# A hybrid decoder layer on one core: a PSUM tile for each accumulating bank, and the last norm's squares summed by TensorE

## The chip, the cores and the metric

One core of a Trainium2 chip runs the whole layer as one program. The metric is device time in microseconds (us) of one execution; a median of several runs is given. The profile is of one further execution. TensorE appears twice in it: PE is the products, PEld the loads of the stationary operand, which overlap them. DVE is VectorE, ACT is ScalarE, POOL is GpSimd, SP issues the DMAs.

## The reference, cut to what matters

512 prompt tokens and 8 single sample tokens pass one layer of width 1024:

```
h = x + Mixer(RMSNorm(x));  h = h + SwiGLU(RMSNorm(h));  y = RMSNorm_final(h)
swiglu(xn) = (silu(xn @ w_a) * (xn @ w_b)) @ w_ffn_out        hidden width 2816
rmsnorm(x, g) = x * rsqrt(mean(x*x over the 1024 features) + eps) * g
```

The change touches the second product of the SwiGLU (with `w_ffn_out`) and the final norm. The mixer (retention, dilated attention, gates) stays as it is.

## The kernel before

Everything is feature-major: a tile holds 128 features on its partitions and 520 columns, which are two halves of 260 (256 prompt tokens and 4 sample tokens each). A float32 product is made of three products of shortened operands: weight and activation are each split into a high and a low part (`wh`, `wl`; `xh`, `xl`), and high·high, high·low and low·high are added in PSUM. ACT makes each `wh` (L195), DVE makes `wl = raw - wh` (L198). `advance(t)` issues these splits up to six blocks ahead of TensorE, in program order; six buffers each for `wh` and `wl` are reused.

PSUM has eight banks. The pool `pmain` has two buffers, tag `pm`, each of shape [128, 2, 512], so two banks a buffer; the pool `pside` has three one-bank buffers for transposes and small sums (`sbank`, tiles named `sp`) and one more bank (`abank`, tag `acc`). The order of the instructions on each engine is the order of the program text; the framework adds the semaphore waits from what tiles the instructions read and write.

**The FFN's second product, first two chunks.** The hidden width is cut into chunks of 8, 8 and 6 tiles. For the first two chunks a pair of 2 x 2 blocks is multiplied with seven products instead of eight (a Strassen-like scheme). `ffn_out(c)` for c = 0, 2, 4, 6 calls `quad` (L268), which runs seven groups of 12 products: 8 calls in all, four behind each chunk. The list `SEVEN` says which PSUM bank each group adds to: 0, 1, 0, 2, 0, 1, 0. Banks 0 and 1 are the two halves of one `pm` tile; bank 2 is the `acc` bank, named `pc`. After groups 1, 2, 3 and 5 ACT copies the bank as it then stands into SBUF (L288, the snapshots `s12`, `s35`); after groups 4, 5, 6 and 7 `evac` has DVE add banks and snapshots into `hT` (L1239 to L1247), the residual stream in SBUF. So a bank is read while its sum is still open, and written again by a later group.

**The last chunk and the final norm.** The last six hidden tiles go through plain products: output tiles c = 0 and 1 interleaved (`LAST`), then 2 and 3 (`unit`, L245), then c = 4 to 7 for the first half of the columns (f = 0) and again for the second (f = 1), at L1354. There a `pm` tile is taken for two values of c, one bank each. `ev_f` (L1323, DVE) adds each result to `hT`.

For the final norm each tile is turned token-major. `fin_T` makes three PE transposes (L307) into two `sp` buffers: 2 x 128 prompt tokens and 4 sample tokens. `fin_sq` squares and sums them on ACT with an accumulator (L1279, L1281: three activations, each with a read of the accumulator). `fin_g` (DVE, L1285, L1287) multiplies by the norm's weight into `yt` and `ys`. A generator `gen_final` does this for one c; `pump`, called after each product step, advances the generators by one step, `drain` runs them to their end. `fin_out(f)` adds the eight partial sums (L1302, L1304), makes 1/rms (`rstd_rows`: DVE L314, a power on POOL, L316), scales `yt` (L1312 on DVE, L1310 on ACT) and issues the output DMAs. The first half's `fin_out(0)` stands with a drain inside the f = 1 pass, the second's at the end.

Of the kernel before, what the change touches and what calls it, by code (L numbers as in the profile page):

```python
# [8 lines left out]
F32 = mybir.dt.float32  # L9
F32R = mybir.dt.float32r  # L10
AF = mybir.ActivationFunctionType
ALU = mybir.AluOpType
AX = mybir.AxisListType
# [4 lines left out]
T, NS, C, D = 512, 8, 520, 1024  # L18
HF, HT = 260, 256
# [13 lines left out]
def tile_hybrid_layer(  # L33
# [9 lines left out]
    V, A, G_, PE, SP = nc.vector, nc.scalar, nc.gpsimd, nc.tensor, nc.sync  # L43
# [5 lines left out]
    pmain = ctx.enter_context(tc.tile_pool(name="pmain", bufs=2, space=PSUM))  # L49
# [39 lines left out]
    ones1 = cst[:, 272:273]  # L89
# [173 lines left out]

    SEVEN = ((0, 0), (1, 3), (0, 4), (2, 1), (0, 5), (1, 2), (0, 6))

    def quad(xh, xl, snap, evac):

        s = pos[0] // 8  # L268
        pos[0] += 16
        nkp = QUADS[s]  # L270
        pm = pmain.tile([128, 2, 512], F32, tag="pm", name="pm")
        out = [pm[:, 0, :HF], pm[:, 1, :HF], None]
        begun = set()
        for j, (bank, x) in enumerate(SEVEN):
            advance(bid[s, 0] + j)
            if bank == 2:
                out[2] = abank("pc")[:, :HF]
            h, l = split[bid[s, 0] + j]
            for k in range(nkp):
                ks = slice(k * 128, k * 128 + 128)  # L280
                for w, r in ((h, xh), (h, xl), (l, xh)):
                    PE.matmul(out[bank], w[:, ks], r[:, k, x, :], start=bank not in begun, stop=k == nkp - 1 and r is xh and w is l,  # L282
                              skip_group_check=True)
                    begun.add(bank)
                if k % 2:
                    pump()
            if j in (0, 1, 2, 4):
                A.activation(snap[(0, 3, 1, None, 2)[j]], out[bank], AF.Copy)  # L288
            evac(j, out[bank])
# [10 lines left out]
    def sbank(name="sp"):  # L300
        return pside.tile([128, 512], F32, tag="s", name=name)

    def abank(name="acc"):
        return pside.tile([128, 512], F32, tag="acc", bufs=1, name=name)
# [6 lines left out]
    def rstd_rows(pool, ssq, rows, ncol, n, tag):  # L311

        v = pool.tile([128, 8], F32, tag=tag + "v", bufs=2, name="v")
        V.tensor_scalar(v[:rows, :ncol], ssq, 1.0 / n, EPS, op0=ALU.mult, op1=ALU.add)  # L314
        r = pool.tile([128, 8], F32, tag=tag + "r", bufs=2, name="r")
        G_.tensor_tensor(r[:rows, :ncol], v[:rows, :ncol], mhalf[:rows].to_broadcast([rows, ncol]), op=ALU.pow)  # L316
        return r
# [14 lines left out]
    sp = sbank("warmup")  # L332
    for i in range(5):
        PE.matmul(sp[:, :256], om[:, :4, :].rearrange("p b m -> p (b m)"), om.rearrange("p b m -> p (b m)"), start=True,
                  stop=True)
# [30 lines left out]
    for k in range(1, 4):  # L366
        sq = tmp("sq")
# [67 lines left out]
    for h in range(RH):  # L435
# [245 lines left out]
        for which in ("q", "k"):  # L681
            e0, e1 = rot(which)
            if h == 0 and which == "q":
                pattern[:] = ["P"]
                push("P", gen_norm1())
                pms = [pmain.tile([128, 2, 512], F32, tag="pm", name="pm") for _ in range(2)]
# [448 lines left out]
    hT = hp.tile([128, 8, C], F32, name="hT")  # L1135
    rs2 = hp.tile([128, C], F32, name="rs2")
    fp = open_pool("fp", "right")
# [5 lines left out]
    def ftmp(name):  # L1143
        return fp.tile([128, C], F32, tag="t", bufs=6, name=name)
# [49 lines left out]
    UH4, UL4 = (u.rearrange("p (k x) c -> p k x c", x=7) for u in (UH, UL))  # L1194
# [36 lines left out]
    def ffn_out(c):  # L1231

        s12 = fp.tile([128, 2, HF], F32, tag="s12", bufs=2, name="s12")
        s35 = fp.tile([128, 2, HF], F32, tag="s35", bufs=2, name="s35")
        h1, h2 = halves(hT[:, c, :]), halves(hT[:, c + 1, :])

        def evac(j, bank):
            if j == 3:
                V.tensor_tensor(h1[:, 0, :], bank, h1[:, 0, :], op=ALU.add)  # L1239
                later(1, lambda: V.tensor_tensor(h1, h1, s12, op=ALU.add))  # L1240
            elif j == 4:
                later(1, lambda: V.tensor_tensor(s35[:, 0, :], s35[:, 0, :], s35[:, 1, :], op=ALU.add))
            elif j == 5:
                V.tensor_tensor(h1[:, 1, :], bank, h1[:, 1, :], op=ALU.add)
                V.tensor_tensor(h2[:, 1, :], h2[:, 1, :], s35[:, 0, :], op=ALU.subtract)
            elif j == 6:
                V.tensor_tensor(h2[:, 0, :], h2[:, 0, :], bank, op=ALU.subtract)  # L1247

        quad(UH4, UL4, [s12[:, 0, :], s12[:, 1, :], s35[:, 0, :], s35[:, 1, :]], evac)

    for (a, n), ahead in zip(CHUNKS, (1, 1, 0)):
        if not ahead:
# [8 lines left out]
    ys = fp.tile([4, 2, D], F32, name="ys")  # L1261
    gb = fp.tile([128, D], F32, name="gb")
    SP.dma_start(gb, lnf.to_broadcast([128, D]))
    ssp = fp.tile([128, 4, 8], F32, name="ssp")
    sss = fp.tile([4, 2, 8], F32, name="sss")

    def fin_T(c, f):
        h = hT[:, c, :]
        sp, sp2 = sbank(), sbank()
        for j in range(2):  # L1270
            o = f * HF + 128 * j
            pe_T(sp[:, j * 128:(j + 1) * 128], h[:, o:o + 128])
        pe_T(sp2[:4, :128], h[:, f * HF + HT:(f + 1) * HF])
        return sp, sp2

    def fin_sq(c, f, sp, sp2):
        for j in range(2):
            junk = ftmp("junk")
            A.activation(junk[:, :128], sp[:, j * 128:(j + 1) * 128], AF.Square, accum_out=ssp[:, 2 * f + j, c:c + 1])  # L1279
        junk = ftmp("junk")  # L1280
        A.activation(junk[:4, :128], sp2[:4, :128], AF.Square, accum_out=sss[:, f, c:c + 1])  # L1281

    def fin_g(c, f, sp, sp2):
        cs = slice(c * 128, (c + 1) * 128)
        V.tensor_tensor(yt[:, 2 * f:2 * f + 2, cs], sp[:, :256].rearrange("p (j c) -> p j c", j=2),  # L1285
                        gb[:, cs][:, None, :].to_broadcast([128, 2, 128]), op=ALU.mult)
        V.tensor_tensor(ys[:, f, cs], sp2[:4, :128], gb[:4, cs], op=ALU.mult)  # L1287

    def gen_final(c, fs=(0, 1)):
        for f in fs:  # L1290
            for _ in range(2 if f else 5):
                yield
            a = fin_T(c, f)
            yield
            fin_sq(c, f, *a)
            fin_g(c, f, *a)
            if f != fs[-1]:
                yield

    def fin_out(f):  # L1300
        s = fp.tile([128, 4], F32, tag="fs", bufs=2, name="fs")
        V.tensor_reduce(s[:, 0:2], ssp[:, 2 * f:2 * f + 2, :], AX.X, ALU.add)  # L1302
        r = rstd_rows(fp, s[:, 0:2], 128, 2, D, "nf")
        V.tensor_reduce(s[:4, 2:3], sss[:, f, :], AX.X, ALU.add)  # L1304
        r4 = rstd_rows(fp, s[:4, 2:3], 4, 1, D, "ng")
        for i in range(2):
            cs = slice(512 * i, 512 * i + 512)
            for j in (2 * f, 2 * f + 1):
                if j % 2:
                    A.activation(yt[:, j, cs], yt[:, j, cs], AF.Copy, scale=r[:, 1:2])  # L1310
                else:
                    V.tensor_scalar(yt[:, j, cs], yt[:, j, cs], r[:, 0:1], None, op0=ALU.mult)  # L1312
                SP.dma_start(y_p[0, j * 128:(j + 1) * 128, cs], yt[:, j, cs])
        V.tensor_scalar(ys[:, f, :], ys[:, f, :], r4[:4, 0:1], None, op0=ALU.mult)
        SP.dma_start(y_s[4 * f:4 * f + 4].rearrange("r o d -> r (o d)"), ys[:, f, :])
# [8 lines left out]

    pattern[:] = ["P"]
    nk = CHUNKS[2][1]
    pms = [pmain.tile([128, 2, 512], F32, tag="pm", name="pm") for _ in range(2)]
    base = pos[0]
    for i, (c, k) in enumerate(LAST):
# [10 lines left out]
    base = pos[0]  # L1340
    for f in range(2):
        for c in range(4, 8):
            if c % 2 == 0:
                pm = pmain.tile([128, 2, 512], F32, tag="pm", name="pm")
            o = pm[:, c % 2:c % 2 + 1, :]
            for k in range(nk):
                n = base + (c - 4) * nk + k
                if f == 0:
                    begin(n)
                h, l = split[bid[n // 8, n % 8 // 4]]  # L1350
                js = slice(n % 4 * 128, n % 4 * 128 + 128)
                xh, xl = (u[:, f * HF:(f + 1) * HF] for u in usrc(k))
                for i, (w, x) in enumerate(((h, xh), (h, xl), (l, xh))):
                    PE.matmul(o[:, 0, :HF], w[:, js], x, start=k == 0 and i == 0, stop=k == nk - 1 and i == 2)  # L1354
                if k % 2:
                    pump()
                if f and c == 4 and k == 3:
                    a = fin_T(7, 0)
                if f and c == 4 and k == 5:
                    fin_sq(7, 0, *a)  # L1360
                    fin_g(7, 0, *a)
                if f and c == 5 and k == 1:
                    drain("P")
                    fin_out(0)
            ev_f(o[:, :, :HF], c, f)
            if c < 7:
                push("P", gen_final(c, (f,)))
    drain("P")
    a = fin_T(7, 1)
    fin_sq(7, 1, *a)  # L1370
    fin_g(7, 1, *a)
    fin_out(1)
    fp.release()
    hp.release()
# [96 lines left out]
```

## Time and profile before

| what | value |
|---|---|
| median of 3 runs | 1347.23 us (1346.02 to 1347.63) |
| the profiled execution's own time | 1344.79 us |
| its span, first to last instruction | 1343.0 us |
| mean granted TensorE clock | 0.997 |
| PE busy | 97% |
| DVE busy | 56% |
| ACT busy | 40% |
| POOL busy | 6% |

A product of 260 columns lasts some 0.28 us from its start to its modelled end, but the next starts about 0.12 us after it: products are pipelined, and a line of the timeline says when one began. What the engine lost in a place is read from the distance of starts, and from the bracket at the end of a line, which gives idle time and what ended it.

### The profile page before, as it was taken

To read this page: it belongs to the slowest core of one execution; us is meant where nothing else is said; L and a number is where in the kernel's file an instruction comes from. 1 tells how busy PE (TensorE), PEld (TensorE's weight loads), DVE (VectorE), ACT (ScalarE), POOL (GpSimd) and SP (SyncE) were. 2 spreads that over 40 slices of the span, in tenths; PEclk is the share of its full clock that TensorE was granted. 3 is DMA by queue.
4 is the path that set the end of the run, shared out by engine and by line. 5 is a ranking of instruction groups with operands and counts; after the bars stand their busy time and mean duration, and the time that the engine had idled before them with its cause. 6 is when DMAs were issued, how large, how long until landed. Compare 5 with 4: busy or idle time off the path is not lost.

```text
span 1343.0 us, 25698 instructions
## 1 busy us (share of the span) xinstructions
PE 1299.2 (97%) x10585; PEld 1259.3 (94%) x10585; DVE 757.6 (56%) x1586; ACT 535.4 (40%) x1068; POOL 83.5 (6%) x69
## 2 busy tenths in 40 slices
PE   8999999998999999999999999999999899989996
PEld 7999999997988999999999999999999799978995
DVE  7867537747655522344444546575556755675444
ACT  4564335535453522334344342343333433343334
POOL 3601001010002000000000000210000000000000
PEclk9999999999999999999999999999999999999999
DMA  6276245647493322445464557243222233233311
GB/s 233 66 264 214 79 143 185 215 150 245 135 316 122 95 88 88 147 142 154 147 185 141 155 158 265 80 139 111 85 89 80 79 95 104 71 88 101 95 48 64
DMA packets 89782, 183.36 MB, mean 137 GB/s; under 512 B 12024, under 2 KB 33944, under 8 KB 89664
## 3 DMA queue, kind: packets, MB, share of 16 engines
q1 hardware_dynamic: 88944, 180.64, 42.2%
q8 instruction: 83, 1.36, 0.4%
q10 hardware_dynamic: 720, 1.07, 0.2%
q14 instruction: 35, 0.29, 0.1%
HBM read 155.70 MB, written 25.98 MB: 135 GB/s over the span
## 4 chain that ended last, share of the span: by engine, by line
PE 88%; DVE 4%; DMA 3%; ACT 2%; issue 1%; POOL 1%; SPq 0%; DVEq 0%; ACTq 0%
PE pm L245 69%; PE pm L282 6%; PE sp L307 2%; DMA vb<-vd 2%; PE sp L536 2%; PE sp L554 2%; PE sp L946 1%; PE pm L1354 1%; PE sp L488 1%; PE pc L282 1%; ACT s L288 1%; DVE wl L198 1%; PE sp L896 1%; PE oacc L649 1%; PE sacc L1091 1%
## 5 line engine op out<-in xcount | busy, mean ns | idle before, releaser
L245 PE MATMUL pm<-X,wh 128*128 128x260 f32 x4608 | 754.2, 285 | 3.9 <-DVE X L339 3.6
L245 PEld LDWEIGHTS pm<-X,wh 128*128 128x128 f32 x4608 | 634.2, 189 | 18.4 <-issue 8.2
L245 PE MATMUL pm<-X,wl 128*128 128x260 f32 x2304 | 464.0, 283 | 0.1
L198 DVE TENSOR_TENSOR wl<-raw,wh 128x512 fp32r<-128x512 f32 x384 | 275.0, 720 | 218.5 <-ACT wh L195 216.5
L245 PEld LDWEIGHTS pm<-X,wl 128*128 128x128 f32 x2304 | 355.2, 188 | 0.5 <-DVE wl L349 0.5
L195 ACT ACTIVATE wh<-raw 128x512 fp32r<-128x512 f32 x384 | 237.9, 625 | 242.6 <-PE pm L245 182.3
L245 PE MATMUL pm<-GA,wh 128*128 128x260 f32 x512 | 82.2, 283 | 0.0
L282 PE MATMUL pm<-UH,wh 128*128 128x260 f32 x192 | 57.6, 300 | 15.6 <-ACT s L288 11.4
L245 PEld LDWEIGHTS pm<-GA,wh 128*128 128x128 f32 x512 | 70.1, 188 | 0.0
L282 PEld LDWEIGHTS pm<-UH,wh 128*128 128x128 f32 x192 | 36.1, 188 | 22.3 <-ACT s L288 16.4
L604 ACT ACTIVATE kv<-vb,ks 128x512 f32<-128x512 f32 x64 | 44.2, 714 | 31.1 <-DMA vb<-vd 30.7
L316 POOL TENSOR_TENSOR r<-v,cst 128x4 f32<-128x4 f32 (+4 forms) x14 | 17.6, 1260 | 621.3 <-DVE fs L1304 399.9
L282 PE MATMUL pm<-UL,wh 128*128 128x260 f32 x192 | 54.2, 282 | 0.0
L282 PE MATMUL pm<-UH,wl 128*128 128x260 f32 x192 | 54.1, 282 | 0.0
L639 DVE SCALAR_TENSOR_TENSOR st<-st,kv 128x512 f32<-128x512 f32 x64 | 45.3, 712 | 12.3 <-ACT kv L604 11.4
L245 PE MATMUL pm<-GA,wl 128*128 128x260 f32 x256 | 51.5, 283 | 0.0
L1209 ACT ACTIVATE fa<-fa 128x520 f32<-128x520 f32 x22 | 14.1, 640 | 71.3 <-DVE fa L1208 71.3
L245 PE MATMUL pm<-M,wh 128*128 128x260 f32 x256 | 41.1, 283 | 0.0
L245 PEld LDWEIGHTS pm<-GA,wl 128*128 128x128 f32 x256 | 39.5, 188 | 0.0
L282 PEld LDWEIGHTS pm<-UL,wh 128*128 128x128 f32 x192 | 36.1, 188 | 0.0
L282 PEld LDWEIGHTS pm<-UH,wl 128*128 128x128 f32 x192 | 36.1, 188 | 0.0
L245 PEld LDWEIGHTS pm<-M,wh 128*128 128x128 f32 x256 | 35.1, 188 | 0.0
(280 smaller groups left out, 1523.5 us busy)
## 6 DMA issues: line engine op xcount, KB each, us to landing
raw<-wall SPq DMA_DIRECT2D x192, 512.0 KB
st<-state SPq DMA_DIRECT2D x64, 256.0 KB
out<-st SPq DMA_DIRECT2D x64, 256.0 KB
area<-ck SPq DMA_DIRECT2D x24, 512.0 KB
vb<-vd SPq DMA_DIRECT2D x32, 256.0 KB
area<-qd SPq DMA_DIRECT2D x12, 512.0 KB
cb<-cd SPq DMA_DIRECT2D x4, 768.0 KB
xr<-xT SPq DMA_DIRECT2D x8, 260.0 KB
```

The lines of the kernel that those rows point to most:

```text
L195: A.activation(h, r, AF.Copy)
L198: V.tensor_tensor(l, r, f32(h), op=ALU.subtract)
L245: PE.matmul(pm[:, f, :HF], w, x[:, f * HF:(f + 1) * HF], start=first, stop=last)
L282: PE.matmul(out[bank], w[:, ks], r[:, k, x, :], start=bank not in begun, stop=k == nkp - 1 and r is xh and w is l, skip_group_check=True)
L288: A.activation(snap[(0, 3, 1, None, 2)[j]], out[bank], AF.Copy)
L307: PE.transpose(out, in_, ident[:n, :n])
L316: G_.tensor_tensor(r[:rows, :ncol], v[:rows, :ncol], mhalf[:rows].to_broadcast([rows, ncol]), op=ALU.pow)
L536: PE.matmul(sp[:, i0:], v[x][:, jb, c * 128:(c + 1) * 128], scs[y][:, SCO[jb]:SCO[jb] + T - i0], start=jb == 0 and x == y, stop=jb == 3 an ...
L554: PE.matmul(sp, kt[x][:, jb, dt * 128:(dt + 1) * 128], v[y][:, jb, :], start=jb == 0 and x == y, stop=jb == 3 and x == 1)
L604: A.activation(kvs[i][:, :DV], vbs[b], AF.Copy, scale=ks[:, dt, b:b + 1])
L639: V.scalar_tensor_tensor(sts[i], sts[i], GAMMA[h], kvs.pop(i)[:, :DV], op0=ALU.mult, op1=ALU.add)
L1209: A.activation(t, t, AF.Silu)
```

## The change

Two edits.

- In `quad` the two accumulating banks become two `pm` tiles, of which only the first bank is used; `odd` (the call's parity) says which of the two is bank 0. In the last chunk's f passes each c takes a `pm` tile of its own in the same way.
- In the final norm ACT squares `hT` feature-major, in one activation for each tile or half, and TensorE sums over the features with a column of ones: for each c and half three products with one column into `ssb`, a bank taken from `abank`. They accumulate there over c. `rstd_rows` reads `ssb` directly, and the tiles `ssp`, `sss` and the two reductions go. The last tile's work for f = 0 moves from the product loop of c = 4 into `fin_out(0)`, and `fin_out(0)` with its drain moves from c = 5 to c = 6 of the f = 1 pass.

```diff
-    def quad(xh, xl, snap, evac):
+    def quad(odd, xh, xl, snap, evac):
...
-        pm = pmain.tile([128, 2, 512], F32, tag="pm", name="pm")
-        out = [pm[:, 0, :HF], pm[:, 1, :HF], None]
+        pms = [pmain.tile([128, 2, 512], F32, tag="pm", name="pm")[:, 0, :HF] for _ in range(2)]
+        out = (pms[::-1] if odd else pms) + [None]
...
-        quad(UH4, UL4, [s12[:, 0, :], s12[:, 1, :], s35[:, 0, :], s35[:, 1, :]], evac)
+        quad(c // 2 % 2, UH4, UL4, [s12[:, 0, :], s12[:, 1, :], s35[:, 0, :], s35[:, 1, :]], evac)
...
-    def fin_sq(c, f, sp, sp2):
+    def fin_ss(c, f, sq):
         for j in range(2):
-            junk = ftmp("junk")
-            A.activation(junk[:, :128], sp[:, j * 128:(j + 1) * 128], AF.Square, accum_out=ssp[:, 2 * f + j, c:c + 1])
-        junk = ftmp("junk")
-        A.activation(junk[:4, :128], sp2[:4, :128], AF.Square, accum_out=sss[:, f, c:c + 1])
+            PE.matmul(ssb[:, 2 * f + j:2 * f + j + 1], sq[:, 128 * j:128 * j + 128], ones1, start=c + f + j == 0, stop=c == 7,
+                      skip_group_check=True)
+        PE.matmul(ssb[:4, 4 + f:5 + f], sq[:, HT:HF], ones1, start=False, stop=c == 7, skip_group_check=True)
...
     def gen_final(c, fs=(0, 1)):
+        sq = ftmp("sqf")
+        A.activation(sq[:, :HF * len(fs)], hT[:, c, HF * fs[0]:HF * fs[-1] + HF], AF.Square)
         for f in fs:
-            for _ in range(2 if f else 5):
+            for _ in range(2 if f else 4):
                 yield
             a = fin_T(c, f)
-            yield
-            fin_sq(c, f, *a)
+            fin_ss(c, f, sq[:, HF * (f - fs[0]):])
+            yield
             fin_g(c, f, *a)
...
     def fin_out(f):
-        s = fp.tile([128, 4], F32, tag="fs", bufs=2, name="fs")
-        V.tensor_reduce(s[:, 0:2], ssp[:, 2 * f:2 * f + 2, :], AX.X, ALU.add)
-        r = rstd_rows(fp, s[:, 0:2], 128, 2, D, "nf")
-        V.tensor_reduce(s[:4, 2:3], sss[:, f, :], AX.X, ALU.add)
-        r4 = rstd_rows(fp, s[:4, 2:3], 4, 1, D, "ng")
+        sq = ftmp("sqf")
+        A.activation(sq[:, :HF], hT[:, 7, f * HF:(f + 1) * HF], AF.Square)
+        a = fin_T(7, f)
+        fin_ss(7, f, sq)
+        r = rstd_rows(fp, ssb[:, 2 * f:2 * f + 2], 128, 2, D, "nf")
+        r4 = rstd_rows(fp, ssb[:4, 4 + f:5 + f], 4, 1, D, "ng")
+        fin_g(7, f, *a)
...
+    ssb = abank("ssb")
...
         for c in range(4, 8):
-            if c % 2 == 0:
-                pm = pmain.tile([128, 2, 512], F32, tag="pm", name="pm")
-            o = pm[:, c % 2:c % 2 + 1, :]
+            o = pmain.tile([128, 2, 512], F32, tag="pm", name="pm")[:, :1, :]
...
-                if f and c == 4 and k == 3:
-                    a = fin_T(7, 0)
-                if f and c == 4 and k == 5:
-                    fin_sq(7, 0, *a)
-                    fin_g(7, 0, *a)
-                if f and c == 5 and k == 1:
+                if f and c == 6 and k == 0:
                     drain("P")
                     fin_out(0)
...
     drain("P")
-    a = fin_T(7, 1)
-    fin_sq(7, 1, *a)
-    fin_g(7, 1, *a)
     fin_out(1)
```

## Rows read from the trace of the kernel before

**Rows 1.** The page: the chain that ended last, shares of the span.

```profile
PE 88%; DVE 4%; DMA 3%; ACT 2%; issue 1%; POOL 1%; SPq 0%; DVEq 0%; ACTq 0%
```

**Rows 2.** Line L282: what ended TensorE's idle time before it (us, times).

```profile
  ACT s L288: 27.9, 48
  DVE hT L1244: 10.0, 16
```

**Rows 3.** Four quads: length; busy PE, PEld, DVE, ACT, POOL; PEclk, DMA share, GB/s.

```profile
1032.29:1084.61 52.32, 44.52 (x338) 41.19 (x337) 37.85 (x64) 22.09 (x44) 0.00 (x0) 1.00 0.33 100
```

**Rows 4.** Timeline of PE, first quad: start us, length us, instruction, [idle before <-releaser].

```profile
1032.29 0.28 PE L282 MATMUL pm<-UH,wh 128*128 128x260 f32 x1
...
1034.36 0.38 PE L282 MATMUL pm<-UH,wh 128*128 128x260 f32 x1 [0.48 <-ACT s L288]
...
1038.09 0.29 PE L282 MATMUL pc<-UH,wh 128*128 128x260 f32 x1
...
1039.53 0.28 PE L282 MATMUL pm<-UH,wh 128*128 128x260 f32 x1
...
1045.37 0.28 PE L282 MATMUL pm<-UH,wh 128*128 128x260 f32 x1
```

**Rows 5.** Timeline of ACT in the first quad: the snapshot behind the third group.

```profile
1038.29 0.39 ACT L288 ACTIVATE s<-pm 128x260 f32<-128x260 f32 x1 [1.27 <-PE pm L282]
```

**Rows 6.** Timeline of DVE: ahead of the first quad; end of the second quad.

```profile
1033.09 0.69 DVE L1214 TENSOR_TENSOR fb<-pm,rs 128x520 f32<-128x520 f32 x1
...
1056.43 0.43 DVE L1244 TENSOR_TENSOR hT<-pm,hT 128x260 f32<-128x260 f32 x1 [0.55 <-PE pm L282]
1056.77 0.42 DVE L1245 TENSOR_TENSOR hT<-hT,s 128x260 f32<-128x260 f32 x1
...
1057.71 0.68 DVE L198 TENSOR_TENSOR wl<-qq,wh 128x512 fp32r<-128x512 f32 x1
```

**Rows 7.** Timeline where the last chunk begins with two new pm tiles: PE, then DVE.

```profile
1286.85 0.40 PE L245 MATMUL pm<-UH,wh 128*128 128x260 f32 x2
...
1287.05 0.70 DVE L1214 TENSOR_TENSOR fb<-pm,rs 128x520 f32<-128x520 f32 x1 [1.44 <-PE pm L245]
```

**Rows 8.** Timeline of PE: products with a column of ones, in three places.

```profile
123.09 0.95 PE L564 MATMUL sp<-cst,ssa 128*128 128x1 f32 x8
123.90 0.73 PE L245 MATMUL pm<-X,wh 128*128 128x260 f32 x4
...
813.17 0.83 PE L1067 MATMUL sp<-cst,ps 128*128 128x1 f32 x6 [0.43 <-DVE ps L1060]
...
932.13 1.05 PE L1175 MATMUL sp<-cst,acc 128*65 128x1 f32 x16
```

**Rows 9.** Timeline of PE, last chunk: first f product, a transpose, the drain, the last product.

```profile
1305.12 0.28 PE L1354 MATMUL pm<-UH,wh 128*128 128x260 f32 x1
...
1310.96 0.49 PE L307 MATMUL sp<-cst,hT 128*128 128x128 f32 x3
1311.21 0.37 PE L1354 MATMUL pm<-UH,wh 128*128 128x260 f32 x1
...
1320.40 0.71 PE L307 MATMUL sp<-cst,hT 128*128 128x128 f32 x5
...
1326.61 0.37 PE L1354 MATMUL pm<-UH,wh 128*128 128x260 f32 x1
...
1333.24 0.28 PE L1354 MATMUL pm<-UH,wl 128*128 128x260 f32 x1
```

**Rows 10.** Timeline of DVE, the tail.

```profile
1333.57 0.43 DVE L1323 TENSOR_TENSOR hT<-pm,hT 128x260 f32<-128x260 f32 x1 [1.01 <-PE pm L1354]
...
1336.07 0.17 DVE L314 TENSOR_SCALAR v<-fs 128x2 f32<-128x2 f32 x1
...
1337.06 0.88 DVE L1312 TENSOR_SCALAR yt<-yt,r 128x512 f32<-128x512 f32 x2 [0.59 <-POOL r L316]
```

**Rows 11.** Busy time in the stretch with the drain (columns as in rows 3).

```profile
1317.00:1327.00 10.00, 6.98 (x45) 4.48 (x44) 5.31 (x17) 7.46 (x53) 0.00 (x0) 1.00 0.00 1
```

More of the change, by code (lines that the diff above doesn't have):

```diff
@@ L1263, in tile_hybrid_layer @@
     SP.dma_start(gb, lnf.to_broadcast([128, D]))
-    ssp = fp.tile([128, 4, 8], F32, name="ssp")
-    sss = fp.tile([4, 2, 8], F32, name="sss")
     def fin_T(c, f):
```

## The prediction

> **What bounds the kernel now.** Read the chain of waits on the page first: 88% of the span's last-ending chain lies on TensorE [rows 1]. So only what shortens TensorE's own time, or the gaps between its products, moves the end. Next, the list of what TensorE waited for at the quads' line: 48 times a snapshot of ACT, 16 times DVE's L1244 [rows 2]. Weight load and product are listed apart, so these are 24 and 8 waits; over eight quads, three and one in each. Third, the timeline of one quad. A group has 12 products at 0.12 us (1038.09 to 1039.53 is 1.44), so group 2 should start at 1032.29 + 1.44 = 1033.73; it starts at 1034.36, with the snapshot as releaser [rows 4]. The snapshot reads bank 0 and group 2 writes bank 1 of the same tile, so the wait follows the tile and not the bank. The counter-check is in the same quad: ACT takes the snapshot behind group 3 at 1038.29 [rows 5], while group 4 has been running since 1038.09, without a bracket, because its bank is another tile (`pc`) [rows 4]. Length of a quad: 52.3 / 4 = 13.08 us [rows 3] for 84 products of 0.12 = 10.08. Each quad thus loses 3.0 us, restarts included.
>
> **Edit 1, the quads.** With a tile for each bank only true waits are left. By `SEVEN`, bank 0 is written in groups 1, 3, 5, 7 and bank 1 in 2 and 6; between a snapshot and the next group on its bank lies always one other group, 1.44 us of products. A snapshot begins when its group's last product has ended and lasts 0.39 [rows 5]; with an ACT split of 0.6 in the way it is still done before 1.44. So the four waits go: 8 x 3.0 = 24.0 us.
>
> What is late next? First DVE: 37.85 us busy in four quads, 9.46 each [rows 3], against 10.08 of products. It stays under, and the sum overstates it: instructions start 0.34 apart that are listed with 0.43 [rows 6]. Its splits run about five groups ahead, so a short delay costs nothing. ACT has 22.09 / 4 = 5.5. DMA had a share of 0.33, which becomes 0.43; loads are issued two quads ahead.
>
> Second, the handover between quads. Both `pm` buffers now belong to one quad, so the next one needs them at once. `odd` swaps the roles: the next group 1 writes the buffer that group 6 left (read by L1244), the next group 2 the one that group 7 left (read by L1247). On DVE, L1244, L1245, one block sum, one split and L1247 stand in that order: starts 1056.43, 1056.77, 1057.11 and 1057.71 give 0.34 + 0.34 + 0.60, then 0.60 for the split and 0.43 for L1247, which ends 2.3 after L1244's start [rows 6]. In the tight schedule I have L1244 starting 0.3 after group 6 ends (a split stands in front of it); L1247 ends 2.6 after that point, and the next group 2 starts two groups, 2.88, after it. Slack 0.2 us there, 2 x 0.7 for group 1. No stall is booked, but this is the tightest place.
>
> Third, the first quad behind each chunk: its bank 1 now takes the buffer that the last unit filled, and DVE's L1214 reads that until 1033.09 + 0.69 = 1033.78 [rows 6], while group 2 wants to start at 1033.73. With the restart 0.2 us, twice: +0.4. That taking two buffers ahead does not hold the first product back is seen in the last chunk: its products begin at 1286.85, before L1214 has read the other buffer at 1287.05 [rows 7]; it also shows that buffers come in rotation, the older first.
>
> Edit 1: -24.0 + 0.4 = -23.6. Bounds: -24.0 without any new wait; if each of the six handovers inside a chunk waits 0.75 (what a wait costs now, 3.0 / 4), -19.1.
>
> **Edit 2, last chunk and final norm.** From the first f product (1305.12) to the last (1333.24) are 28.12 us [rows 9]. 143 steps of 0.12 are 17.2; twelve visits of `fin_T` lie in between at 0.25 each (1310.96 to 1311.21), 3.0. The other 7.9 is waiting: in the drain 1320.40 to 1326.61 = 6.2, less seven visits of 0.25, makes 4.5; the rest is c = 5 and 7 waiting for the evacuation of their sister bank, and visits that wait for `hT` or an `sp` buffer. In the drain ACT is the busier engine (7.46 of 10 us, against PE 6.98 and DVE 5.31 [rows 11]): two `sp` buffers are held until three squares and their accumulator reads are done. These squares leave the path: ACT now squares `hT` before, without waiting for TensorE. I keep 0.6 for restarts that stay, and take -7.3.
>
> Added on TensorE, in line: three products with one column for each visit. Each is two instructions: four calls took 123.90 - 123.09 = 0.81, 0.20 each [rows 8]. The third call loads four columns only; I set 0.1, so 0.5 a visit. Bounds: 0.13 a call as with 65 columns (1.05 / 8), 0.39 a visit; 0.28 a call as three took from a standing start (0.83 / 3), 0.83 a visit. The nearest row is the 128-column one within running products, hence 0.5. Counting steps: nine pumps a generator now (ten before), 31 pumps to the later drain, so six visits lie before it, eight in it with `fin_out(0)`, two after the last product; 14 as before the last product. 14 x 0.5 = +7.0 (5.5 to 11.6). In the drain a visit is then 0.75 on TensorE; DVE's two products by the weight are what frees the buffers, and ACT needs 0.4 a square. I add 0.3 for waits there.
>
> Moved: `fin_out(0)` issues five DMAs some 5.7 us before the last five (33 products of 0.12, and the longer chain at the end); nothing else is on SP's queue then. Its scalings wait on DVE for POOL's power, and c = 6's evacuation stands behind them; c = 7 writes the other buffer, so only the visit behind c = 7 needs it, 33 products later.
>
> Tail: before, from the last evacuation (1333.57) to `v` (1336.07) 2.50, then 0.99 to the scaling [rows 10]. After: evacuation 0.43, square 0.39 (the size of a snapshot), three products 0.5, result 0.25, handovers 0.1: 1.7 to `v`. The two reductions go too. -0.8; the second part stays.
>
> Edit 2: -7.3 + 7.0 + 0.3 - 0.8 = -0.8, bounds -2.3 and +3.8. TensorE's products for the sums about eat what the waits give back.
>
> **Sum.** -23.6 - 0.8 = -24.4. The profiled execution (1344.79, span 1343.0) becomes 1320.4, span 1318.6. The median of the runs lies 2.4 above the profiled one; carried along, 1347.23 - 24.4 = 1322.8.
>
> **Rivals.** (a) The handover between quads binds: L1247 late on DVE, 0.75 at each of six places, 1327.3. For: slack of 0.2, DVE 94% busy. Against: its busy time counts overlaps. (b) The one-column products cost 0.83 a visit, +4.6: 1327.4. For: an fp32 stationary operand loaded for one column leaves nothing to hide the load. Against: they stand within running products. (c) The change doesn't do what it says, the waits in the quads stay because they hang on ACT's order and not on the tile: 1347.23 - 0.8 = 1346.4, no change. Against: group 4 doesn't wait [rows 4, 5].
>
> (d) TensorE's clock falls to the 1.2 GHz level in the last chunk, since the drain is now transposes and one-column products alone. From the drain on this doubles 33 products (+4.0) and at most the drain's 6 us: 1333. It ends slower than before only if the half clock holds for more than 24.4 us of the chunk's 46 (1286.85 to 1333.24 [rows 7, 9]); over all of it 1322.8 + 46 = 1369. Against: the old drain, seven visits and 4.5 us of waiting, was granted 1.00 throughout [rows 11]. The Trainium skill bears on this rival: "TensorE: Matmul & The Clock Gate", Part 4: PE-mode transpose, has it that transposes don't count as work for the clock gate, and the table in "Why this matters for your kernels" that an idle stretch brings half rate back. By that rule the old drain should already have shown it; the trace differs, and the measurement decides.
>
> **How the numbers follow.** Forecast 0.79 (own range 1319.5 to 1326), (a) 0.08, (b) 0.08, (c) 0.03, (d) 0.02. Best sum -24.0 - 2.3 = -26.3, 1320.9; with the spread of the medians (1346.0 to 1347.6) the range begins at 1319, and it ends at 1328 to take in (a) and (b), not both. About 0.2% (2.7 us) is what can be told from no change. All cases but (c) and half of (d) are faster beyond it: 0.96; same 0.03; slower 0.01.
>
> **What would show it.** In the changed profile: a quad of 10.1 us, no ACT snapshot among the releasers of L282, at most two waits on L1214 at the second group; if group 1 or 2 of a later quad names L1244 or L1247, (a) holds. Visits of 0.75 in the drain with one-column products, PEclk 1.00 there, the last product about as long after 1286.85 (less 23.6) as now, and 1.7 us from the last evacuation to `v`. The forecast is wrong if quads stay above 11 us, or the last chunk takes 3 us more or less than now.

## The result, and the profile after

The changed kernel takes 1324.83 us, median of four runs (1322.27 to 1326.96), against 1347.03 (1346.02 to 1347.63) for the kernel before: a ratio of 0.9835, 95% interval 0.9814 to 0.9857, or 22.2 us less. Its profiled execution, one of the four, took 1326.3 (span 1324.5, mean granted clock 0.994).

Landmarks of the PE timeline divide both spans (the stretches between, which the change leaves as they were, are left out); the last row is a second profiled execution of the same program, which an experiment below gave (`e3_no_swap`):

| profiled execution | start to first quad | eight quads | last chunk's first product to first f product | f products, first to last | last product to end | span |
|---|---|---|---|---|---|---|
| before | 1032.29 | 104.68 | 18.27 | 28.12 | 9.76 | 1343.0 |
| after | 1033.14 | 81.26 | 19.58 | 31.63 | 9.00 | 1324.5 |
| after, second execution | 1033.30 | 81.25 | 19.58 | 28.63 | 8.95 | 1321.6 |

The quads gave 23.4 us. The last chunk and the tail took back 1.0 in one execution and 4.1 in the other.

**The quads.** First four quads of after: length; busy PE, PEld, DVE, ACT, POOL; PEclk, DMA share, GB/s. It answers to [rows 3].

```profile
1033.14:1073.77 40.63, 40.58 (x339) 40.41 (x337) 36.16 (x64) 22.14 (x44) 0.00 (x0) 1.00 0.39 118
```

52.32 became 40.63, 10.16 a quad, with PE busy for all but 0.05 of the 40.63. What ended TensorE's idle time at the quads' line, now L283, answers to [rows 2]:

```profile
its engine sat idle before it (us, times) until:
  issue: 0.5, 2
```

The 48 waits for a snapshot and the 16 for L1244 (after: L1245) have gone; two stalls are left. The PE timeline of the first quad shows one of them, at the second group:

```profile
1034.46 0.28 PE L283 MATMUL pm<-UH,wl 128*128 128x260 f32 x1
1034.79 0.36 PE L283 MATMUL pm<-UH,wh 128*128 128x260 f32 x1
```

where the next start is 0.33 away instead of 0.12. The profile names no releaser there ("issue"); DVE's timeline shows what fits: the last unit's bank is read until 1033.94 + 0.70 = 1034.64, 0.15 before the second group starts. At the other stall, in the fifth quad, the same read ends 0.14 before it.

```profile
1033.94 0.70 DVE L1215 TENSOR_TENSOR fb<-pm,rs 128x520 f32<-128x520 f32 x1
```

The handover from the first quad to the second, on which rival (a) turns, DVE and then PE:

```profile
1044.26 0.42 DVE L1248 TENSOR_TENSOR hT<-hT,pm 128x260 f32<-128x260 f32 x1
...
1047.83 0.28 PE L283 MATMUL pc<-UH,wh 128*128 128x260 f32 x1
```

**The last chunk.** What TensorE waited for, from the last chunk's first product to the end, before:

```profile
PE sp L307 <- DVE yt L1285: 2.8, 7, 0.9
PE pm L1354 <- DVE hT L1323: 1.3, 3, 0.6
PE sp L307 <- DVE hT L1323: 0.5, 2, 0.3
```

The same view of after is empty: not one wait is listed. Yet the stretch became longer. The products by line of after, 1264.3 to 1324 (busy us, mean ns | idle before), say with what the time was filled:

```profile
L1277 PE MATMUL ssb<-cst,sqf 128*128 128x1 f32 x64 | 8.4, 236 | 0.0
L1279 PE MATMUL ssb<-cst,sqf 128*4 128x1 f32 x32 | 3.1, 165 | 0.0
```

These are 96 instructions with one column, six in each of 16 visits, 14 of which lie ahead of the last product. A visit is the work on one tile and half: the transposes and the one-column products. The first among the f products, in after's PE timeline:

```profile
1284.58 0.49 PE L308 MATMUL sp<-cst,hT 128*128 128x128 f32 x3
1284.91 0.50 PE L1277 MATMUL ssb<-cst,sqf 128*128 128x1 f32 x4
1285.34 0.19 PE L1279 MATMUL ssb<-cst,sqf 128*4 128x1 f32 x2
1285.46 0.39 PE L1355 MATMUL pm<-UH,wh 128*128 128x260 f32 x1
```

It holds TensorE from 1284.58 to 1285.46, 0.88 us; the others outside the drain take 0.88 to 0.89. Two visits of the drain in after's PE timeline, the last one, and the products behind it (compare [rows 9]):

```profile
1301.98 0.55 PE L308 MATMUL sp<-cst,hT 128*128 128x128 f32 x3
1302.37 0.50 PE L1277 MATMUL ssb<-cst,sqf 128*128 128x1 f32 x4
1302.80 0.19 PE L1279 MATMUL ssb<-cst,sqf 128*4 128x1 f32 x2
1302.92 0.55 PE L308 MATMUL sp<-cst,hT 128*128 128x128 f32 x3
...
1307.62 0.82 PE L308 MATMUL sp<-cst,hT 128*128 128x128 f32 x3
1308.24 0.85 PE L1277 MATMUL ssb<-cst,sqf 128*128 128x1 f32 x4
...
1309.52 0.42 PE L1355 MATMUL pm<-UL,wh 128*128 128x260 f32 x1
1309.74 0.42 PE L1355 MATMUL pm<-UH,wl 128*128 128x260 f32 x1
```

A visit here is 1301.98 to 1302.92, 0.94 us. The last of the eight takes 1.52, and the products behind it start 0.22 apart instead of 0.12. Why is read from the granted clock (columns as above; PEclk is the third figure from the end):

```profile
1307.00:1308.00 1.00, 1.00 (x11) 0.90 (x9) 0.61 (x2) 0.00 (x0) 0.00 (x0) 0.88 0.00 0
1308.00:1309.00 1.00, 1.00 (x7) 0.97 (x4) 0.00 (x0) 0.00 (x0) 0.00 (x0) 0.50 0.00 0
...
1314.00:1315.00 1.00, 1.00 (x8) 1.00 (x7) 0.00 (x0) 0.00 (x0) 0.00 (x0) 0.71 0.57 219
```

TensorE was granted half its clock, 1.2 GHz, from 1307.8 to 1314.6. That cost 0.58 in the last visit and some 24 products x 0.1 behind it: 3.0 us, the difference between the f products of the two executions (31.63 and 28.63).

**The tail.** DVE after the last evacuation, to be read beside [rows 10]:

```profile
1315.82 0.43 DVE L1325 TENSOR_TENSOR hT<-pm,hT 128x260 f32<-128x260 f32 x1 [2.60 <-PE pm L1355]
...
1317.59 0.21 DVE L315 TENSOR_SCALAR v<-ssb 128x2 f32<-128x2 f32 x2 [0.82 <-PE ssb L1279]
...
1318.56 0.88 DVE L1314 TENSOR_SCALAR yt<-yt,r 128x512 f32<-128x512 f32 x2 [0.23 <-POOL r L317]
```

1.77 to `v` instead of 2.50, then 0.97 to the scaling.

### The profile page after: what moved, and what is told of

It reads as the page before. It is cut to its first block, busy times and chain, and to the rows that moved or that the text cites. A ratio compares the mean times of both kernels' runs of the same rounds, so it can differ in the third digit from the quotient of the medians.

```text
span 1324.5 us, 25798 instructions
## 1 busy us (share of the span) xinstructions
PE 1303.2 (98%) x10681; PEld 1272.9 (96%) x10681; DVE 753.6 (57%) x1582; ACT 527.1 (40%) x984; POOL 83.6 (6%) x69
## 4 chain that ended last, share of the span: by engine, by line
PE 89%; DVE 4%; DMA 3%; issue 1%; ACT 1%; POOL 1%; SPq 0%; DVEq 0%; ACTq 0%
PE pm L245 70%; PE pm L283 5%; PE sp L308 3%; DMA vb<-vd 2%; PE sp L537 2%; PE sp L555 2%; PE pm L1355 2%; PE sp L947 1%; PE sp L489 1%; PE pc L283 1%; DVE wl L198 1%; PE sp L897 1%; PE sacc L1092 1%; DVE X L408 0%; PE sp L886 0%
## 5 line engine op out<-in xcount | busy, mean ns | idle before, releaser
L283 PE MATMUL pm<-UH,wh 128*128 128x260 f32 x192 | 54.4, 283 | 0.1
L283 PE MATMUL pm<-UH,wl 128*128 128x260 f32 x192 | 54.3, 283 | 0.0
L283 PE MATMUL pm<-UL,wh 128*128 128x260 f32 x192 | 54.3, 283 | 0.0
L283 PEld LDWEIGHTS pm<-UH,wh 128*128 128x128 f32 x192 | 36.2, 189 | 0.5 <-issue 0.5
L283 PEld LDWEIGHTS pm<-UL,wh 128*128 128x128 f32 x192 | 36.2, 188 | 0.0
L283 PEld LDWEIGHTS pm<-UH,wl 128*128 128x128 f32 x192 | 36.1, 188 | 0.0
L865 DVE SCALAR_TENSOR_TENSOR area<-area 128x128 f32<-128x128 f32 x96 | 22.7, 290 | 22.5 <-DMA area<-qd 22.5
```

What stands on the lines that cost most here:

```text
L865: V.scalar_tensor_tensor(pr[:, e], kb[:, e], 1.0, qb[:, e], op0=ALU.mult, op1=ALU.mult, accum_out=Ss[:, g, 32 * h + b:32 * h + b + 1])
```

## The experiments

The first four ran on one chip (before there: 1346.28, 11 runs), the other four in a second session (before there: 1347.64, 9 runs). Ratios are to the kernel before of the same session.

**The tiles alone** (`e1_tiles_only`): before, with a tile for each bank in the quads and in the f passes; the norm stays.

```diff
+        pms = [pmain.tile([128, 2, 512], F32, tag="pm", name="pm")[:, 0, :HF] for _ in range(2)]
+        out = (pms[::-1] if odd else pms) + [None]
...
+            o = pmain.tile([128, 2, 512], F32, tag="pm", name="pm")[:, :1, :]
```

> Edit 1 alone (tiles of their own in the quads and in the f passes; the final norm as before). Theory A (the quads' tiles carry the whole gain, the norm's edit is about even or costs a little): the quads give 23.4 us as in the changed kernel's trace, the f passes at most 2 more: 1321.5 to 1324 against 1347.0, the granted clock 0.996 or more in every run because the drain is the old one. Rival B (the norm's edit earned some us of the gain): 1326 or more.

Measured: 1321.45 (1318.54 to 1323.32), ratio 0.9809 (0.979 to 0.9828): lower than the whole change's 1324.94 in the same session (`e3_no_swap`, after's program), with intervals that overlap at their edge. The clock was not what theory A expected: its mean was 0.992 to 0.996 in the four runs, and not 0.996 or more in each. The quads take 81.21. The f products take 26.63, of which about 1.4 is a half-rate stretch (1303.7 to 1307.1), so 25.2 against 28.12. The drain is the old one, with its waits and then half-rate products, 0.22 apart. PE, and the granted clock in one microsecond of it:

```profile
1303.62 1.23 PE L307 MATMUL sp<-cst,hT 128*4 128x128 f32 x4 [0.38 <-DVE yt L1285]
...
1304.86 0.42 PE L1352 MATMUL pm<-UL,wh 128*128 128x260 f32 x1
```

```profile
1304.00:1305.00 1.00, 1.00 (x5) 0.62 (x5) 0.63 (x2) 0.73 (x5) 0.00 (x0) 0.50 0.02 8
```

What follows: the sister-bank waits of the f passes, which the prediction booked within edit 2, are worth some 2.9 us (28.12 - 25.2) and belong to the tiles. (In the next kernel, which shares the banks, TensorE still waits four times there, 2.1 us.)

**The norm alone** (`e2_norm_only`): after, with the shared tiles put back.

```diff
-        pms = [pmain.tile([128, 2, 512], F32, tag="pm", name="pm")[:, 0, :HF] for _ in range(2)]
+        pm = pmain.tile([128, 2, 512], F32, tag="pm", name="pm")
+        out = [pm[:, 0, :HF], pm[:, 1, :HF], None]
...
+            if c % 2 == 0:
+                pm = pmain.tile([128, 2, 512], F32, tag="pm", name="pm")
+            o = pm[:, c % 2:c % 2 + 1, :]
```

> Edit 2 alone (squares summed by TensorE, drain at c = 6), quads and f passes on the old shared tiles. Theory A: not faster than before: 1348 to 1350 in runs without a clock dip (14 visits of 0.55 us more against the old drain's waits), about 3 us more in runs with a dip in the drain (granted clock about 0.003 lower). Rival (my sum on record for this edit, -0.8, or better): 1346 or less.

Measured: 1353.78 (1351.13 to 1356.53), ratio 1.0051 (1.0032 to 1.007): 0.5% slower than before, clear of the noise, and more than theory A's 1348 to 1350 (1351 to 1353 with a fall of the clock). Quads 104.65 as before; last chunk to first f product 19.57 (+1.3), f products 34.64, tail 8.97. Its drain lost the clock as well, in the seventh visit:

```profile
1333.00:1334.00 1.00, 1.00 (x13) 0.93 (x11) 0.67 (x3) 0.00 (x0) 0.00 (x0) 1.00 0.00 0
1334.00:1335.00 1.00, 1.00 (x8) 0.87 (x8) 0.51 (x2) 0.00 (x0) 0.00 (x0) 0.68 0.00 0
```

What follows: the whole gain is the tiles', and the new norm costs. On top of the tiles it costs 3.5 us in the medians (1324.94 of the next experiment, the changed program, against 1321.45), alone 7.5. The profiles say what the 7.5 holds. The last chunk with its tail takes 63.18 here against 56.15 before, 7.0 more: 1.0 is what after's undisturbed execution has too (57.16), 3.0 is the half-rate stretch (the last two visits at 1.60 each, then products 0.22 apart), and the rest, 3.0, is the four sister-bank waits with their restarts, which stay here and are gone in after. How much of the 3.0 for the clock each of the six runs paid stays open.

**No exchange of the roles** (`e3_no_swap`): after, with `odd` always 0.

```diff
-        quad(c // 2 % 2, UH4, UL4, [s12[:, 0, :], s12[:, 1, :], s35[:, 0, :], s35[:, 1, :]], evac)
+        quad(0, UH4, UL4, [s12[:, 0, :], s12[:, 1, :], s35[:, 0, :], s35[:, 1, :]], evac)
```

> The changed kernel with odd always 0, so that the first group of a quad writes the bank that the seventh group before it left. Theory (a true wait of about 0.75 us then stands at each of the six handovers inside a chunk): 4 to 5 us more than the changed kernel (1324.8), so 1329, with L1247 as releaser six times. Rival (DVE's slack hides it): 1325, no wait on L1247.

Measured: 1324.94 (1323.42 to 1329.13), ratio 0.9842 (0.9822 to 0.9862), the same as after. The quads take 81.25, no wait at a handover, and the order of the instructions is after's on every engine. The two kernel files give the same program: in both, every product writes the same PSUM bank, and the first group of a quad gets the buffer that group 6 of the quad before it left, whatever `odd` says; only names of tiles differ. So `odd` decides nothing, the theory rested on a wrong reading of it, and the run does not test the handover. It gave something else, a further profiled execution of after's program, with a drain that the clock did not fall in:

```profile
1308.00:1309.00 1.00, 1.00 (x11) 0.93 (x10) 0.18 (x3) 0.00 (x0) 0.00 (x0) 1.00 0.00 0
```

The drain is then eight visits in 7.46 us (1301.25 to 1308.71), and the last chunk with its tail 57.16 against 56.15 before. It is the undisturbed measure of edit 2 used here.

**Visits spread** (`e4_spread`): after, with a pump after every step and the drain three steps later.

```diff
-                if k % 2:
-                    pump()
-                if f and c == 6 and k == 0:
+                pump()
+                if f and c == 6 and k == 3:
```

> The changed kernel with the generators pumped after every product step of the f passes instead of every second, and the drain three steps later: about 3 visits are left in the drain instead of 8, the same work. Theory C (the clock falls because the drain keeps TensorE for 8 us on transposes and one-column products alone): no dip at the drain in the profile, granted clock 0.996 or more in every run, 1321 to 1322.5 and a spread under 2 us. Rival D (the dip comes by chance as the one at 18 us did, whatever the drain): some runs again at 0.993 to 0.994 and 1326.

Measured: 1326.48 (1324.86 to 1327.73), ratio 0.9848 (0.9831 to 0.9865): no gain, and neither the spread (2.9) nor the granted clock (0.991 to 0.996) came out as theory C had it. The drain shrank to three visits (1307.80 to 1310.57), but `fin_out(0)` came so late that its scalings stood on DVE ahead of an evacuation. DVE:

```profile
1312.46 0.74 DVE L1316 TENSOR_SCALAR ys<-ys,r 4x1024 f32<-4x1024 f32 x1
1313.13 0.41 DVE L1325 TENSOR_TENSOR hT<-pm,hT 128x260 f32<-128x260 f32 x1
```

and TensorE, held behind it at a transpose, with the half-rate starts a little later (0.22 apart from 1315.30):

```profile
1313.59 0.55 PE L308 MATMUL sp<-cst,hT 128*128 128x128 f32 x3 [0.96 <-DVE hT L1325]
...
1315.30 0.42 PE L1355 MATMUL pm<-UH,wh 128*128 128x260 f32 x1
```

As a test of the clock it decides nothing: the fall came at 1315.1, behind three visits, some 2 us of products, 0.96 us of waiting and one more visit, so no single cause stands alone.

**A long drain** (`e5_long_drain`): after, with no visit handed out in the f passes.

```diff
                 if k % 2:
-                    pump()
+                    run_delayed()
```

> The changed kernel, but the visits wait for each other: in the f passes nothing is pumped between products, so some twelve visits (transposes and one-column products) instead of seven follow each other in the drain without a product of 260 columns among them. The number of visits and products is the same. Theory A (TensorE's clock falls to its half level when such visits stand alone for long enough, by chance at six microseconds): a stretch of 11 us falls in every execution, the visits at its end and the products behind it run at half speed, the drain and the products after it take 4 to 8 us more than in the undisturbed changed kernel, 1326 to 1331, and the profile shows a granted clock of 0.5 in the drain. Theory B (what was seen in the drain has nothing to do with the visits; it falls as often anywhere): no more dips than before; only the waits of visits that stand together cost, 0.06 us for each of five, 1324 to 1326.

Measured: 1329.71 (1324.48 to 1332.32), ratio 0.986 (0.9838 to 0.9883). Twelve visits stand in the drain, 1298.48 to 1312.10. The first transposes of four visits in its PE timeline, where the clock falls, and the granted clock there:

```profile
1305.00 0.55 PE L308 MATMUL sp<-cst,hT 128*128 128x128 f32 x3
...
1305.94 0.65 PE L308 MATMUL sp<-cst,hT 128*128 128x128 f32 x3
...
1307.30 0.90 PE L308 MATMUL sp<-cst,hT 128*128 128x128 f32 x3
...
1308.90 0.90 PE L308 MATMUL sp<-cst,hT 128*128 128x128 f32 x3
```

```profile
1306.00:1307.00 1.00, 1.00 (x8) 0.98 (x7) 0.67 (x3) 0.00 (x0) 0.00 (x0) 0.63 0.00 0
1307.00:1308.00 1.00, 1.00 (x8) 0.87 (x8) 0.03 (x1) 0.00 (x0) 0.00 (x0) 0.50 0.00 0
```

A visit goes from 0.94 to 1.60 while PE is busy all the time, and the clock comes back at 1316.4 only, among the products. The f products take 32.80, 4.2 more than undisturbed. So theory A holds for size and place in this profile, and the median lies in its range. Its "every execution" is not shown: one profile shows the fall; of the five runs four have a mean granted clock of 0.987 to 0.990, and the fifth, 1324.48, has 0.995.

**The squares added up on POOL** (`e6_acc`): four sums by TensorE instead of sixteen.

```diff
+        sq = ftmp("sqf") if c else accs
+        cs = slice(HF * fs[0], HF * fs[-1] + HF)
+        A.activation(sq[:, cs], hT[:, c, cs], AF.Square)
+        if c:
+            G_.tensor_tensor(accs[:, cs], accs[:, cs], sq[:, cs], op=ALU.add)
...
-            fin_ss(c, f, sq[:, HF * (f - fs[0]):])
...
+        fin_ss(0, f, accs[:, f * HF:(f + 1) * HF])
```

> The changed kernel, but the squares of the eight feature tiles are first added up on POOL into one tile, and TensorE sums only that and the last tile's: four visits with one-column products instead of sixteen. Theory A (the one-column products, 0.55 us of TensorE's time in each of fourteen visits before the last product, are what the second edit costs): twelve visits become 0.5 shorter, less 1 us that the drain then waits for DVE's reading of the transposes; some 4 to 5 us less than the changed kernel, 1319 to 1321. Theory B (the last chunk is bound by waits, for the evacuations and the sp buffers, and the products only fill them): within 1 us of the changed kernel, 1323 to 1326.

Measured: 1319.08 (1315.91 to 1320.41), ratio 0.9782 (0.9766 to 0.9798), faster than after (0.9835, 0.9814 to 0.9857). By landmarks 18.26 + 24.27 + 9.44 = 51.97, 5.2 less than the undisturbed 57.16. That is theory A: TensorE's sums are the cost. Below them lies DVE, busy without a gap from 1300 to 1303, which now paces the drain's visits, one every 0.58 us:

```profile
1300.34 0.42 DVE L1285 TENSOR_TENSOR yt<-sp,gb 128x256 f32<-128x256 f32 x1
...
1300.88 0.42 DVE L1285 TENSOR_TENSOR yt<-sp,gb 128x256 f32<-128x256 f32 x1
...
1301.48 0.42 DVE L1285 TENSOR_TENSOR yt<-sp,gb 128x256 f32<-128x256 f32 x1
```

**The same, paced** (`e7_acc_paced`): the squares on POOL as before it, a pump after every step, with shorter pauses in the generator to match, drain and `fin_out(0)` at c = 5.

```diff
...
-            for _ in range(2 if f else 4):
+            for _ in range(3 if f == 0 else 2 if f == fs[0] else 1):
...
-                if k % 2:
-                    pump()
-                if f and c == 6 and k == 0:
+                pump()
+                if f and c == 5 and k == 0:
```

> As the kernel with the squares added up on POOL, but the visits are handed out after every step of the f passes, and the rest with the first half's norm stands in the middle of the second pass at c = 5, so that hardly a visit stands in the drain. Theory A (the drain is where the last chunk loses: its visits wait for each other there, and the clock may fall): 1 to 2 us less than without the pacing, 1317.5 to 1319.5, no half-rate stretch in the last chunk in any profile. Theory B (visits cost the same wherever they stand): same as without the pacing within 0.7 us.

Measured: 1317.25 (1316.41 to 1319.72), ratio 0.9775 (0.976 to 0.979). The median is 1.8 lower, but the intervals overlap almost wholly, and the landmarks sum to 51.31, 0.66 less than unpaced: nearer to theory B, and not told apart from no gain. In the profiles of both the clock stays at 1.00 up to the last product, so they do not say either whether pacing spares the fall. This kernel, the unpaced one and the next are the fastest of the study, and I can't rank the three.

**The old norm, paced** (`e8_old_paced`): the tiles alone, with the same pacing and pauses.

```diff
-                if k % 2:
-                    pump()
-                if f and c == 4 and k == 3:
+                pump()
+                if f and c == 5 and k == 0:
+                    drain("P")
                     a = fin_T(7, 0)
-                if f and c == 4 and k == 5:
+                if f and c == 5 and k == 2:
...
```

> The first edit alone with the old norm (squares and accumulator reads on ACT, token-major), but its visits are handed out after every step of the f passes, as in the kernel with the paced sum, and the first half's norm follows at c = 5. Theory A (the old norm's cost was the drain, where visits wait for ACT to free the sp buffers): the first f product to the last takes 22 to 23 us instead of 25 to 27, and the kernel 1317.5 to 1320, 2 to 4 less than the first edit alone (1321.45). Theory B (ACT's squares bind wherever the visits stand): within 1 us of 1321.45.

Measured: 1318.68 (1315.94 to 1320.89), ratio 0.9781 (0.9765 to 0.9798). The f products take 23.70, 1.5 less than the tiles alone without their half-rate stretch; theory A had 22 to 23. Waits are left, in another mix (before: the list under "The last chunk"). What TensorE waited for up to the last product:

```profile
PE sp L307 <- DVE hT L1323: 1.6, 3, 0.9
PE sp L307 <- DVE yt L1285: 0.9, 1, 0.9
```

The gain has the sign and somewhat less than the size of theory A. In the runs it can't be told: the interval overlaps that of the tiles alone (0.979 to 0.9828).

## Why the prediction was right, and where it was wrong

The forecast, 1322.8, lies 2.0 under the measured 1324.83 and inside what the interval allows (1322.0 to 1327.8). The span of the profiled execution misses by more, 1324.5 against 1318.6. The 5.9 are: the start 0.85 (code that the change doesn't touch; among other differences after has a half-rate stretch at 17.5 to 20.9 us there, before has none); the quads 0.2; the last chunk with its tail 1.8 undisturbed; the fall of the clock in the drain 3.0. The medians hide part of this, because before's median lies 2.2 above its profiled time and after's 1.5 below; that the medians meet to 2.0 is in this part luck. By the prediction's own sign ("the last chunk takes 3 us more or less than now") the profiled execution is outside it: 51.2 from the chunk's first product to the last against 46.4, 4.8 more. Undisturbed it is 48.2, 1.8 more.

- **Edit 1, the quads: right.** -23.4 against -23.6. All four waits a quad went. The third point (L1214, now L1215) came as worked out: two stalls at the second group, 0.28 each with the restart instead of 0.2.
- **The handover between quads (rival a): did not bind.** No releaser at any of the six places. That `odd` swaps the roles of the buffers was misread: the program is the same with `odd` always 0, and the order of buffers that the prediction worked with comes from the pool. In the first handover L1248, the former L1247, starts at 1044.26 behind a split and is through at 1044.68; the second quad's fourth group begins at 1047.83, so its second at 1047.83 - 2 x 1.44 = 1044.95. The slack is 0.27, where the forecast had 0.2.
- **Edit 2, the waits that go: right.** -7.3 booked. Before: 28.12 less 143 x 0.12 and twelve visits of 0.25 is 7.96. After, undisturbed: 28.63 less 17.16, four visits of 0.89 and 7.46 of drain is 0.45. That is -7.5.
- **Edit 2, the sums by TensorE: the step that failed, by its size.** "14 x 0.5 = +7.0", with 0.3 of waits, 7.3. Measured: six visits outside the drain cost 0.89 instead of 0.25 (+3.8), eight in it 7.46 / 8 = 0.93 instead of 0.25 (+5.5): +9.3, or 0.66 a visit, between the 0.5 taken and the 0.83 of rival (b). Of the drain's 0.94 the 128-column calls take 0.43 (1302.37 to 1302.80), near the 0.4 that their row gave [rows 8], the four-column one 0.12, where 0.1 was set without a row, and the transposes 0.39 instead of 0.25. The prediction took the visit's 0.25 from a place with products of 260 columns on both sides. With a one-column product behind them the three transposes hold TensorE 0.33 (1284.58 to 1284.91), and in the drain, where one also stands ahead of them, 0.39. So of the 2.3 that the 7.0 lacked, the transposes make 1.6 (6 x 0.08 + 8 x 0.14) and the sums 0.7 (14 x 0.05); the 0.3 of waits did not come. So edit 2 comes to -7.5 + 9.3 - 0.8 = +1.0 where -0.8 was forecast. Without the sister-bank part, which the tiles alone give, the new norm costs 57.16 - 53.3 = 3.8 (53.3 is the last chunk with the tail in the tiles alone, 54.7, less the 1.4 of the half rate).
- **The tail: right**, 0.8.
- **Rival (d), the clock: wrongly dismissed.** It had 0.02, because the old drain was granted 1.00 [rows 11], and 1.00 was named as a sign for the new one. That was one execution. The old drain lost the clock too (the tiles alone, 1303.7), and the changed one lost it in one profile and kept it in another of the same program. The price is 3.0 and not the 10 of that rival, because the fall came at the end of the drain and the clock was back at 1314.6, among the products behind.

Settled: the gain is the tiles' (23.4 in the quads, 2.9 in the f passes); the norm's sums by TensorE are a loss, since every one-column product is TensorE's time in line, while the waits it removed can be had otherwise (0.978 with the sums on POOL or with the old norm paced, 0.9835 with the change). Open: how often the drain of each kernel loses the clock.

## What to carry to other kernels

Two banks that are written and read in turn should be tiles of their own wherever waits follow tiles: 32 waits of 0.75 us with the restart, less two new stalls of 0.28, were 23.4 us here. On the engine that bounds the kernel, a wait removed by an instruction added is no gain until the instruction is priced in the very neighbourhood where it will stand. A stretch that one profile shows at full clock is not shown to be safe; ask for it twice.

## What the runs showed of the hardware that was not expected

The granted clock of the same program differs from one execution to the next. In the drain of after it fell to 0.50 behind 6.7 us of transposes and one-column products with PE busy at 1.00, and in the second execution it stayed at 1.00 through 7.46 us of the same. Other half-rate stretches stand between 16 and 24 us in nine of the ten profiles (not in before's), between 58 and 63 us in three, and between 332 and 341 us in all ten. The Trainium skill, "TensorE: Matmul & The Clock Gate", Part 4: PE-mode transpose, says that a transpose doesn't count as a busy TensorE for the gate in the way that a matmul does. The falls in after (1307.8), in the norm alone (1334.4) and in the long drain (1306.3) agree with that, though one-column products stand between the transposes there and no run tells the two apart; the second execution shows that the same drain need not bring one.
